# Hybrid encoder block: the output projection's weights in a pool of their own, both right-hand pools waiting tile by tile

## Chip, cores and metric

The kernel runs on one core of one Trainium2 chip. The metric is the time of one execution on the device, in microseconds (us); the figure before is the median of three runs.

## What is computed

One layer of a streaming encoder over 2,048 tokens with 16 learned tokens ahead of them, width 1,024, float32. Three groups of heads read the same normalised input: a gated linear recurrence, a forgetting attention (8 heads of 64) and an RWKV-7 recurrence. Their outputs are put side by side and go through one output projection; a feed-forward part follows.

```python
p = rms_norm(h, norm_mix_pre) @ w_in
mixed = concatenate([rg_lru(p[a]), forgetting_attention(p[b]), rwkv7(p[c])]) @ w_out
h = h + rms_norm(mixed, norm_mix_post)
f = causal_dwconv(rms_norm(h, norm_ffn_pre) @ ffn_up, ffn_conv)
gate, val = split(f)
h = h + rms_norm((gelu(gate) * val) @ ffn_down, norm_ffn_post)
```

## The kernel before

The program is traced in the order of the code, and a scheduler puts each engine's instructions into one fixed order; at run time each engine follows its row of instructions and waits with semaphores. All loads and stores of this part are issued by SP, in one row.

The stages follow each other: input projection with the recurrences beside it (to about 1120 us), forgetting attention (about 900 to 1540 us), output projection (from 1200 us beside the attention, to 1650 us), feed-forward up (to about 2460 us) and down.

**Attention** (class `Attn`, L446 to L860). A step is one head and 512 queries. `maxima` (L542) multiplies queries with keys into `mx` (L566), and VectorE reduces each `mx` to maxima (L571); this runs two steps ahead of the rest. `weights` (L661) computes the scores `sc` (L693, L694), ScalarE makes the exponentials `p` out of them (L698, nine buffers), TensorE multiplies them with the values into `po` (L716), and POOL (GpSimd) adds them up in `acc` (L737, two buffers; each fourth addition is VectorE's). At the end of a step `acc` is split (L769, L770), summed over the partitions on TensorE (L772, L773), copied to its first row (L774), and SP writes that row of 512 denominators to DRAM (L775, `scr_den<-acc`). It comes back as a small tile `dcol` (L776), is inverted, written (L781) and read as `rb` (L782); the scaled output is written to `scr_mix` (L786). So an `acc` is free for the step after next when its L775 has left it.

**Output projection.** `w_out_load` (L1508) loads the weights, already split into two halves of float32r (`woh` and `wol`), with sixteen loads of 512 KB. `w_out_tile` (L1519) takes one tile of tokens: `load_parts` (L163) loads the mixed heads into `raw` (L167), ScalarE rounds them to `mh` (L168), VectorE takes the rest `ml` (L169), and `mm3` (L172) multiplies in three products (L174 to L176) into `pswo`. The first tile (tile 0) has only two tokens. Tiles 0 to 6 run beside the attention; tiles 7 and 8 are held behind the step before the last of the attention.

**Memory.** SBUF is given out from both sides. On the right lie, during the first stage, the recurrences' buffers (`gp`, `rp`). During the attention a tile `pad` of 95,488 bytes a partition, which nothing writes, holds that place, and the attention's last tiles (`mt`, `k2`) lie further in. When `pad`'s pool is closed, `g_post` (4 KB a partition) and the pool `wp` are laid from the right edge: `woh` and `wol` (32 KB each), `mh` and `ml` (two of 4 KB each), `raw` (4 KB), `wx` (two of 4 KB) and smaller ones, in all some 5 KB more than `pad` with `g_post` counted in. A pool that is opened plainly waits as a whole for everything that lay in its place before; one opened with `early` (`reuse_waits: "tile"`) has each tile wait only for what lay in that tile's own place.

Of the kernel before, what the change touches and what calls it, by code (L numbers as in the profile page):

```python
# [329 lines left out]
def scratch(tc, ctx, core):  # L330
    dr = ctx.enter_context(tc.tile_pool(name="scr", bufs=1, space=DRAM))
    scr = {
        "p": dr.tile([A_ROWS + C_ROWS, PAD + T], F32, name="scr_p"),
        "v": dr.tile([T, 512], F32, name="scr_v"),
        "f": dr.tile([8, T], F32, name="scr_f"),
        "ch": dr.tile([8, T], F32, name="scr_ch"),
        "cl": dr.tile([8, T], F32, name="scr_cl"),
        "den": dr.tile([8, T], F32, name="scr_den"),
        "rden": dr.tile([8, T], F32, name="scr_rden"),
        "mix": dr.tile([D, T], F32, name="scr_mix"),  # L340
        "h": dr.tile([T, D], F32, name="scr_h"),
        "ff": dr.tile([FF, SEQ], F32, name="scr_ff"),
        "part": dr.tile([SEQ, D], F32, name="scr_part"),
        "us": dr.tile([NFF, P, 4 * 512], F32, name="scr_us"),
        "wo": dr.tile([KD, 2, P, D], F32, name="scr_wo"),
        "wk": dr.tile([3 * D // P + 1, 2, P, D], F32, name="scr_wk"),
        "ds": dr.tile([DOWN_PAIRS, P, 4 * 512], F32, name="scr_ds"),
    }
    for s in ("qh", "ql", "kh", "kl"):
        scr[s] = dr.tile([512, T], F32, name="scr_" + s)  # L350
    return scr
# [1156 lines left out]
def w_out_load(core, pool, scr):  # L1508

    nc = core.nc  # L1510
    wh = pool.tile([P, KD, D], F32R, tag="woh", name="woh", bufs=1)
    wl = pool.tile([P, KD, D], F32R, tag="wol", name="wol", bufs=1)
    for k in range(KD):
        for i, t in enumerate((wh, wl)):
            nc.sync.dma_start(t[:, k].bitcast(F32), scr["wo"][k, i])
    return wh, wl
# [578 lines left out]
def hybrid_block_kernel(ctx: ExitStack, tc: tile.TileContext, args, out):  # L2095
    a = {s: v[0] if s != "meta_tokens" else v for s, v in args.items()}
    nc = tc.nc
    core = Core(tc, ctx)
    scr = scratch(tc, ctx, core)
# [8 lines left out]
    def pool(es, name, bufs, **kw):  # L2108
        return es.enter_context(tc.tile_pool(name=name, bufs=bufs, **kw))

    right = {"side": "right"}
    early = {"reuse_waits": "tile"}

    def spread(pl, vec, name):
        t = pl.tile([P, D], F32, tag=name, name=name)
        nc.sync.dma_start(t[:], vec.rearrange("(o n) -> o n", o=1).broadcast_to([P, D]))
        return t
# [3 lines left out]
    with ExitStack() as p1:  # L2121
# [65 lines left out]
        p2 = ExitStack()  # L2187
# [9 lines left out]
    with ExitStack() as p3:  # L2197
        ps_n = pool(p3, "ps_n", 2, space=PSUM, **early)
        ps_f = [pool(p3, "ps_f0", 3, space=PSUM, **early)]
        np_ = pool(p3, "np", 3, **early)  # L2200
        tmp = pool(p3, "tmp", RAWS, **early)
        g_fpre = spread(gf, a["norm_ffn_pre"], "g_fpre")
        uw = [pool(p3, "uw0", UWA, **early)] * UWA
        xo = [pool(p3, f"xo{i}", 1, **early) for i in range(3)]
        tiles = [
            [(i, f, r) for i, (f, r) in enumerate(FFN_TILES) if f < FBLK * 2 * s + FBLK + FN and f + r > FBLK * 2 * s]
            for s in range(SUPERS)
        ]
        rs = {}
        with p2:  # L2210
            ps_wo.append(pool(p2, "ps_wo2", 1, space=PSUM, **right))

            banks = Banks(core, [(ps_f[0], "up", 3), (ps_wo[0], "wo", 2), (ps_wo[1], "wo", 1)])
            g_post = spread(pool(p2, "gpost", 1, **right), a["norm_mix_post"], "g_post")
            wp = pool(p2, "wp", 2, **right)
            core.apart = True
            w = w_out_load(core, wp, scr)
            todo = list(tiles[0])
            quarters = {0: ffn_quarters(core, qp, 0)}
            for i, (f, rows) in enumerate(FFN_TILES):  # L2220
                with tc.issue_after(at.steps[-2].ins) if i in HELD else nullcontext():
                    rs[i] = w_out_tile(
                        core, wp, banks, scr, w, x, meta, g_post, f + META - HALO, rows,
                        rsv[:, 6 * i : 6 * i + 6] if i < len(FFN_TILES) - 1 else None,
                        (core.acted, at.reduced) if i == HELD[-1] + 1 else (),
                    )
                banks.wide = core.root = i >= LATE - 1
                core.apart = not core.root
                if i == LATE:
                    with tc.issue_after(core.finished.ins):  # L2230
                        at.later.pop()[2]()
                for _ in range(NORMS if i > LATE else 0):
                    if todo:
                        q, f, rows = todo.pop(0)
                        xt = ffn_fetch(core, np_, scr, f, rows)
                        ffn_norm(core, ps_n, xt, f, rows, rs[q], g_fpre, quarters[0], 0)
                        if not todo:
                            run(ffn_sums(core, quarters[0]))
        ps_f.append(pool(p3, "ps_f1", 3, space=PSUM, **early))
        uw += [pool(p3, "uw1", UWB, **early)] * UWB  # L2240
        xo += [pool(p3, f"xo{i}", 1, **early) for i in range(3, XO)]
        up = pool(p3, "up", 2, **early)

        sums, ws, down, fetched = [iter(())], {}, [], []

        def fetch():
            if todo:
                q, f, rows = todo.pop(0)
                fetched.append((q, f, rows, ffn_fetch(core, np_, scr, f, rows)))

        def slot():
            down.append(down.pop(0))
            home = down[-1]
            return home.tile([P, 2, 512], F32R, tag="dw", name=core.n("dw")) if hasattr(home, "tile") else home

        def between(sup, j):

            for _ in range(1 + (j % 4 == 3) if sup else 0):
                next(later, None)
            sup += 1  # L2260
            if j == 1 and sup < SUPERS:
                quarters[sup] = ffn_quarters(core, qp, sup)
                todo[:] = tiles[sup]
                fetch()
            elif j == 1:
                kept = qp.tile([P, DOWN_KEPT, 2, 512], F32R, tag="q", name=core.n("qd"))
                down.extend(kept[:, i] for i in range(DOWN_KEPT))
                down.append(gf.tile([P, 2, 512], F32R, tag="g_fpre", name=core.n("kd"))[:])
            elif sup == SUPERS:
                if j in DOWN_FROM:  # L2270
                    raw = lambda: tmp.tile([P, 512], F32, tag="uq", name=core.n("raw"))[:]
                    k = DOWN_FROM.index(j)
                    some = range(min(len(DOWN_PRODUCTS), len(down) - len(DOWN_PRODUCTS) * k))
                    ws[k] = down_operands(core, raw, slot, a["ffn_down"], scr, k, some)
            elif fetched:
                q, f, rows, xt = fetched.pop(0)
                fetch()
                behind = lambda: tc.issue_after(core.conved.ins)
                if rs[q] is None:
                    junk = ps_n.tile([P, 512], F32, tag="mm", name=core.n("psj"))  # L2280
                    v = rsv[:rows, 6 * q : 6 * q + 6]
                    sums_ = v[:, 4:5], v[:, 5:6]
                    for half, acc in enumerate(sums_):
                        with tc.issue_after(core.taken.ins):
                            nc.scalar.activation(
                                junk[:rows], xt[:rows, 512 * half : 512 * half + 512], AF.Square, accum_out=acc
                            )
                    with behind():
                        rs[q] = rstd_root(core, v, sums_, D)
                ffn_norm(core, ps_n, xt, f, rows, rs[q], g_fpre, quarters[sup], sup, behind)  # L2290
                if not fetched:
                    sums.append(ffn_sums(core, quarters[sup], lambda: tc.issue_after(core.pooled.ins)))
            else:
                for _ in range(2):
                    next(sums[-1], None)

        later = down_sums(core, tmp, a["ffn_down"], scr, lambda: tc.issue_after(core.pooled.ins))
        ffn_up(
            core, tmp, uw, up, ps_f, a["ffn_up"], cw, scr, between,
            lambda sup, i: ffn_operand(core, xo, quarters[sup], i),  # L2300
        )
# [78 lines left out]
```

## Time and profile before

| | |
|---|---|
| runs (three) | 2991.94, 2995.55, 2996.49 us |
| median | 2995.55 us |
| span of the profiled execution | 2994.3 us |
| PE busy in the span | 2898.0 us (97%) |
| granted TensorE clock, mean | 0.976 |
| first weight load of the output projection issued | 1166.72 us |
| first matmul of the output projection | 1199.97 us |

Times in the profile count from the start of the span. PE is TensorE's matmuls, PEld its weight loads, DVE is VectorE, ACT ScalarE, POOL GpSimd, SPq the queue of SP. A line such as L716 is the line of the kernel; the tile names have their numbers left out. In a timeline a row begins with its start and its duration, and the bracket at its end has the idle time of the engine before it and what ended that. The profiled execution's own time isn't listed beside its span; the span lies inside the runs.

### The profile page before, as it was taken

Reading aid. Unit: us, or ns where it says so; the run is one execution under the profiler, and the core shown is the slowest. Engines: PE = TensorE matmul, PEld = TensorE weight load, DVE = VectorE, ACT = ScalarE, POOL = GpSimd, SP = SyncE. Lnnn points to the kernel's source line nnn. Section 1 sums busy time; section 2 is a strip of 40 time slices with the busy share of each in tenths; the row PEclk is TensorE's granted clock in tenths of the full one; section 3 lists DMA queues with packets and bytes.
Section 4 is the critical chain, followed back from the end, with each engine's and each line's share of the span. In section 5 each row is a group of like instructions: output and inputs, shape, how many; then the busy total and the mean of one; then the engine's idle time right before and its main releaser. Section 6 shows DMA issues by size and latency. Waiting matters only on the chain.

```text
span 2994.3 us, 52802 instructions
## 1 busy us (share of the span) xinstructions
PE 2898.0 (97%) x18694; PEld 2486.3 (83%) x18694; DVE 2037.0 (68%) x3937; ACT 1480.8 (49%) x2858; POOL 1319.7 (44%) x1567
## 2 busy tenths in 40 slices
PE   6999999999999999999999999999999999999998
PEld 6998899888886655665568999999999999787887
DVE  5258644765677776565636998898778787656766
ACT  4246332443346554455634656666565665424333
POOL 1002122121223665666843667446655544656443
PEclk9999899999988999999999999999999999999999
DMA  6777469676644347544336565577777764436453
GB/s 210 239 235 226 135 230 310 203 242 194 199 129 101 95 109 208 134 113 109 77 96 212 183 198 179 173 220 211 208 208 218 222 198 128 158 116 220 145 174 120
DMA packets 469190, 530.49 MB, mean 177 GB/s; under 512 B 85710, under 2 KB 355736, under 8 KB 467372
## 3 DMA queue, kind: packets, MB, share of 16 engines
q1 hardware_dynamic: 468156, 526.17, 58.2%
q8 instruction: 147, 2.41, 0.3%
q0 software_dynamic: 768, 0.93, 0.1%
q14 instruction: 119, 0.97, 0.1%
HBM read 368.07 MB, written 158.90 MB: 176 GB/s over the span
## 4 chain that ended last, share of the span: by engine, by line
PE 59%; DVE 4%; POOL 2%; DMA 2%; ACT 2%; issue 2%; SPq 0%; DVEq 0%; POOLq 0%; ACTq 0%
PE psu L174 9%; PE psu L175 9%; PE psu L176 9%; PE po L716 4%; PE psd L174 4%; PE psd L175 4%; PE psd L176 4%; PE mx L566 2%; PE pswo L174 2%; PE pswo L176 2%; PE pswo L175 2%; PE sc L693 2%; PE sc L694 2%; POOL acc L737 1%; DVE mc L571 1%
## 5 line engine op out<-in xcount | busy, mean ns | idle before, releaser
L175 PE MATMUL psu<-xo,uw 128*128 128x344 f32 x1848 | 591.4, 320 | 0.0
L174 PE MATMUL psu<-xo,uw 128*128 128x344 f32 x1848 | 586.0, 322 | 2.7 <-ACT u L1828 1.2
L176 PE MATMUL psu<-xo,uw 128*128 128x344 f32 x1848 | 581.9, 320 | 1.3 <-POOL uw L1657 1.0
L174 PE MATMUL psp<-xh,wh 128*128 128x384 f32 (+2 forms) x1152 | 380.8, 331 | 0.0
L176 PE MATMUL psp<-xh,wl 128*128 128x384 f32 (+2 forms) x1152 | 378.0, 328 | 0.0
L175 PE MATMUL psp<-xl,wh 128*128 128x384 f32 (+2 forms) x1152 | 377.8, 328 | 0.0
L1657 DVE TENSOR_TENSOR uw<-uq,uw 128x512 fp32r<-128x512 f32 x341 | 320.3, 944 | 59.2 <-ACT uw L1656 56.7
L174 PEld LDWEIGHTS psu<-xo,uw 128*128 128x128 f32 x1848 | 345.8, 188 | 4.3 <-DVE vb L1848 1.8
L176 PEld LDWEIGHTS psu<-xo,uw 128*128 128x128 f32 x1848 | 345.7, 188 | 2.1 <-POOL uw L1657 1.3
L175 PEld LDWEIGHTS psu<-xo,uw 128*128 128x128 f32 x1848 | 347.1, 188 | 0.0
L1656 ACT ACTIVATE uw<-uq 128x512 fp32r<-128x512 f32 x462 | 287.9, 627 | 95.7 <-PE psu L176 44.4
L698 ACT ACTIVATE p<-sc,bias 128x512 f32<-128x512 f32 (+4 forms) x352 | 197.9, 590 | 142.3 <-PE sc L694 119.2
L571 DVE TENSOR_REDUCE mc<-mx 128x1 f32<-128x512 f32 (+6 forms) x352 | 190.0, 565 | 113.6 <-PE mx L566 80.1
L1796 DVE SCALAR_TENSOR_TENSOR uy<-psu,ffn_cols,uy 128x342 f32<-128x342 f32 (+1 forms) x390 | 220.4, 567 | 61.4 <-ACT uy L1794 59.7
L1804 POOL TENSOR_TENSOR uy<-uy,uy 128x342 f32<-128x342 f32 (+1 forms) x132 | 146.5, 1110 | 229.2 <-DVE uy L1796 55.9
L737 POOL TENSOR_TENSOR acc<-acc,p 128x512 f32<-128x512 f32 (+3 forms) x208 | 222.7, 1073 | 48.4 <-DVE acc L737 23.4
L1657 POOL TENSOR_TENSOR uw<-uq,uw 128x512 fp32r<-128x512 f32 x121 | 184.4, 1524 | 133.8 <-ACT uw L1656 116.0
L174 PEld LDWEIGHTS psp<-xh,wh 128*128 128x128 f32 x1152 | 220.1, 191 | 8.7 <-issue 7.3
L176 PEld LDWEIGHTS psp<-xh,wl 128*128 128x128 f32 x1152 | 220.1, 191 | 7.0 <-issue 5.1
L175 PEld LDWEIGHTS psp<-xl,wh 128*128 128x128 f32 x1152 | 220.1, 191 | 5.0 <-issue 3.2
L1657 DVE TENSOR_TENSOR fo<-u,fo 128x896 fp32r<-128x896 f32 x88 | 101.6, 1155 | 133.7 <-ACT fo L1656 133.2
L1656 ACT ACTIVATE fo<-u 128x896 fp32r<-128x896 f32 x88 | 81.2, 923 | 206.6 <-PE psd L176 118.1
(488 smaller groups left out, 6409.4 us busy)
## 6 DMA issues: line engine op xcount, KB each, us to landing
uq<-scr_us SPq DMA_DIRECT2D x220, 256.0 KB
uq<-in_ffn_up_dram SPq DMA_DIRECT2D x209, 256.0 KB
wl<-scr_wk SPq DMA_DIRECT2D x48, 512.0 KB
wh<-scr_wk SPq DMA_DIRECT2D x48, 512.0 KB
u<-scr_ff SPq DMA_DIRECT2D x88, 256.0 KB
scr_ff<-uy SPq DMA_DIRECT2D x110, 171.0 KB
raw<-in_w_in_dram SPq DMA_DIRECT2D x24, 512.0 KB
scr_wk<-wh SPq DMA_DIRECT2D x24, 512.0 KB
```

Of the source, the lines that this page charges most:

```text
L174: nc.tensor.matmul(out, ah, bh, start=first, stop=False, skip_group_check=more)
L175: nc.tensor.matmul(out, ah, bl, start=False, stop=False, skip_group_check=more)
L176: nc.tensor.matmul(out, al, bh, start=False, stop=last, skip_group_check=more)
L566: nc.tensor.matmul(ps[:rows, : e - a], q3[:, qo : qo + rows], k2[:, a:e], start=True, stop=not last)
L571: self.reduced = nc.vector.tensor_reduce(mc[:rows, i, ci : ci + 1], ps[:rows, : e - a], axis=AX.X, op=ALU.max)
L698: last = nc.scalar.activation(p[:rows, :w], ps[:rows, :w], AF.Exp, bias=bias[:rows, j : j + 1])
L716: mm = nc.tensor.matmul(po[at : at + 64, c0:n], v1[:rows, j], p[:rows, : n - c0], start=start and i < 2, stop=end and i + 2 >= len(group), ...
L737: eng.tensor_tensor(a, ps_[0][0][:rows, c0:n] if start and i == 1 else a, p[:rows, : n - c0], op=ALU.add)
L1656: core.nc.scalar.activation(hi, src, AF.Copy)
L1657: (eng or core.nc.vector).tensor_tensor(lo, src, hi, op=ALU.subtract)
L1796: core.conved = stt(y[:, :n], src[:, i : n + i], cw[:, 44 * i + cc : 44 * i + cc + 1], y[:, :n], op0=ALU.mult, op1=ALU.add)
L1804: core.pooled = nc.gpsimd.tensor_tensor(v[:, :n], g[:, :n], v[:, :n], op=ALU.mult)
```

## The change

The weights get a pool `woh` of their own, laid right behind `g_post`, and both it and `wp` wait tile by tile.

```diff
             g_post = spread(pool(p2, "gpost", 1, **right), a["norm_mix_post"], "g_post")
-            wp = pool(p2, "wp", 2, **right)
+            wo = pool(p2, "woh", 1, **right, **early)
+            wp = pool(p2, "wp", 2, **right, **early)
             core.apart = True
-            w = w_out_load(core, wp, scr)
+            w = w_out_load(core, wo, scr)
```

The sizes stay the same. What changes is what the loads wait for, and with it the order that the scheduler finds. On SP's row of DMA issues, at the place behind `g_post`, stood before (`den` holds denominators, `rb` and `dcol` are their way back, `v`, `q` are values and queries of coming steps):

```order
L2116 DMA g_post<-in_norm_mix_post_dram 128x1024
L782 DMA rb_12986<-scr_rden 64x512
L782 DMA rb_13057<-scr_rden 64x512
L775 DMA scr_den<-acc_12884 1x512
L776 DMA dcol_13044<-scr_den 16x32
L786 DMA scr_mix<-o_12734 64x512
L535 DMA v_1455_11124<-scr_v 128x16x64
L536 DMA v_1455_11124<-scr_v 16x64
L553 DMA q_1446_11103<-scr_qh 64x512
L775 DMA scr_den<-acc_13128 1x512
```

The same place on SP in the changed kernel, from the second `rb` on:

```order
L782 DMA rb_13057<-scr_rden 64x512
L1515 DMA woh<-scr_wo 128x1024
L1515 DMA wol<-scr_wo 128x1024
L1515 DMA woh<-scr_wo 128x1024
L1515 DMA wol<-scr_wo 128x1024
L1515 DMA woh<-scr_wo 128x1024
L1515 DMA wol<-scr_wo 128x1024
L1515 DMA woh<-scr_wo 128x1024
L1515 DMA wol<-scr_wo 128x1024
L775 DMA scr_den<-acc_12884 1x512
```

Eight loads stand ahead of the write of `acc_12884`; the other eight follow behind it, without any row between them. Behind those SP goes on so, to the operand of the first output tile (`raw`):

```order
L553 DMA q_1446_11103<-scr_qh 64x512
L786 DMA scr_mix<-o_12734 64x512
L775 DMA scr_den<-acc_13128 1x512
L786 DMA scr_mix<-o_12818 64x512
L776 DMA dcol_13044<-scr_den 16x32
L652 DMA scr_mix<-mt_13273 64x8x16
L535 DMA v_1455_11124<-scr_v 128x16x64
L536 DMA v_1455_11124<-scr_v 16x64
L553 DMA q_1451_11114<-scr_qh 64x512
L776 DMA dcol_13144<-scr_den 16x32
L167 DMA raw_16463<-scr_mix 128x8x2
```

So the second row of denominators (`acc_13128`) now stands behind all sixteen loads, and `raw` behind it and a load of values.

On TensorE the two orders part behind the last product of the 16 learned tokens (L635). Before, the row goes on with scores:

```order
L635 MATMUL mx_13194<-mt_12912,mt_12913 16x16
L693 MATMUL sc_13311<-q_1974_12943,k_1448_11109 128x512
L694 MATMUL sc_13311<-q_1457_11129,k_1963_12902 128x512
L566 MATMUL mx_13179<-k_1963_12902,q_1446_11103 128x512
L693 MATMUL sc_13316<-q_1974_12943,k_1448_11109 128x512
L694 MATMUL sc_13316<-q_1457_11129,k_1963_12902 128x512
```

In the changed kernel the same score, `sc_13311`, follows after 19 other rows of TensorE, maxima (`mx`) of coming steps among them; the last of those rows are:

```order
L566 MATMUL mx_13297<-k_1449_11110,q_1451_11114 128x512
L566 MATMUL mx_13304<-k_1449_11110,q_1451_11114 128x400
L566 MATMUL mx_13341<-k_1449_11110,q_1451_11114 128x384
L568 LDWEIGHTS identb
L568 MATMUL mx_13341<-futureb,identb 128x128
L566 MATMUL mx_13338<-k_1449_11110,q_1451_11114 128x512
L693 MATMUL sc_13311<-q_1974_12943,k_1448_11109 128x512
L694 MATMUL sc_13311<-q_1457_11129,k_1963_12902 128x512
```

Maxima have moved ahead of scores. Counted from behind that L635, the first output matmul (`pswo`) stands after 78 rows of TensorE in place of 182. POOL's row keeps its order here: the first sum `acc_13237<-p,p`, which takes the place of `acc_12884`, stands behind the same additions in both. From output tile 7 on to the end of the output projection TensorE's row is the same in both; in the feed-forward part some groups of matmuls change places.

## Prediction

> **What bounds the kernel now.** I read the page first. Matmuls fill the span, and the chain that ended last runs on the same engine:
>
> ```profile
> span 2994.3 us, 52802 instructions
> PE 2898.0 (97%) x18694; PEld 2486.3 (83%) x18694; DVE 2037.0 (68%) x3937; ACT 1480.8 (49%) x2858; POOL 1319.7 (44%) x1567
> PE 59%; DVE 4%; POOL 2%; DMA 2%; ACT 2%; issue 2%; SPq 0%; DVEq 0%; POOLq 0%; ACTq 0%
> ```
>
> The edit adds and removes no matmul, so it can act only through idle time of PE (TensorE). Next I cut the span into stretches around the moved loads (columns: stretch, length, then busy time of PE, PEld, DVE, ACT, POOL, granted clock, DMA share, GB/s):
>
> ```profile
> 1150.00:1200.00 50.00, 48.49 (x244) 27.02 (x241) 34.44 (x68) 30.59 (x54) 38.01 (x41) 1.00 0.78 246
> 1200.00:1500.00 300.00, 297.38 (x1352) 178.76 (x1351) 185.08 (x365) 160.48 (x289) 214.78 (x285) 1.00 0.45 107
> 1500.00:1550.00 50.00, 44.18 (x184) 26.60 (x184) 12.68 (x25) 18.99 (x36) 29.25 (x47) 0.97 0.19 53
> 1151.00:1163.00 12.00, 12.00 (x71) 7.08 (x69) 6.50 (x15) 8.35 (x16) 9.05 (x12) 1.00 0.36 79
> 1168.00:1190.00 22.00, 20.92 (x95) 10.93 (x94) 16.34 (x30) 11.75 (x21) 17.23 (x19) 1.00 1.02 375
> ```
>
> Between 1150 and 1200 PE is idle for 1.5 us, in the 300 us behind that for 2.6 us. The DMA engines have room where the loads will go (0.36 of the DMA engines at 1151 to 1163) and full where the loads lie now (1.02, 375 GB/s). Last I read SP's queue and the engine that waits for it, POOL, in order of time (start, duration, instruction, and in brackets the idle time before it and what ended it):
>
> ```profile
> 1145.33 1.09 SPq L782 DMA_DIRECT2D rb<-scr_rden  x2
> 1146.52 0.39 SPq L775 DMA_DIRECT2D scr_den<-acc  x1
> ...
> 1166.72 0.53 SPq L1515 DMA_DIRECT2D woh<-scr_wo  x1
> 1167.30 0.42 SPq L1515 DMA_DIRECT2D wol<-scr_wo  x1
> 1167.81 0.24 SPq L775 DMA_DIRECT2D scr_den<-acc  x1
> ...
> 1184.90 0.32 SPq L1515 DMA_DIRECT2D wol<-scr_wo  x1
> 1185.49 0.84 SPq L167 DMA_DIRECT2D raw<-scr_mix  x1
> ```
>
> ```profile
> 1148.55 1.27 POOL L737 TENSOR_TENSOR acc<-p,p 128x512 f32<-128x512 f32 x1 [0.73 <-DMA scr_den<-acc]
> 1149.90 2.63 POOL L737 TENSOR_TENSOR acc<-acc,p 128x512 f32<-128x512 f32 x2
> ...
> 1159.66 1.27 POOL L737 TENSOR_TENSOR acc<-p,p 128x512 f32<-128x512 f32 x1
> ...
> 1171.97 1.28 POOL L737 TENSOR_TENSOR acc<-p,p 128x512 f32<-128x512 f32 x1 [0.49 <-DMA scr_den<-acc]
> ```
>
> The reader is to see a loop that is easily missed. There are two accumulators `acc`. POOL may start an attention step's sum only when the row of denominators of the step before last (L775, 2 KB) has left its `acc`. Issued at 1146.52 into an empty queue, that write freed POOL at 1148.55, after 2.0 us. Issued at 1167.81 behind two of the weight loads, it freed POOL at 1171.97, after 4.2 us: 1.1 us more for each load ahead. The window 1168 to 1190 gives 0.524 MB / 375 GB/s = 1.4 us for a load. So a small write on this queue waits for the bulk before it.
>
> **The change, part by part.** *The pools.* The split moves no bytes and adds no instruction; its cost is only what it moves. *The loads.* By the order of SP, the sixteen loads go from 1166.72 to 1184.90 to right behind the two rb loads of 1145.33, some 20 us earlier, and with one other row between them. Eight of them now stand ahead of the denominators' write that was issued at 1146.52, all sixteen ahead of the next one. Issuing costs nothing in itself (0.3 to 0.6 us each, SP has nothing else to do then); the cost is what is queued behind them.
>
> *First term: POOL and the exponentials.* With eight loads ahead, the write lands at 1146.5 + 2.0 + 8 x 1.1 to 1.4 = 1157.3 to 1159.7; I take 1158.9 (1.3 each). Then comes POOL's first sum (1.27 us), which frees two buffers `p`, and ScalarE's exponential of the next score, which waits for just that today:
>
> ```profile
> 1149.85 1.26 ACT L698 ACTIVATE p<-sc,bias 128x512 f32<-128x512 f32 x2 [3.38 <-POOL acc L737]
> ...
> 1150.59 0.50 PE L693 MATMUL sc<-q,k 128*128 128x512 f32 x1 [0.43 <-ACT p L698]
> ...
> 1199.97 0.39 PE L174 MATMUL pswo<-woh,mh 128*2 128x512 f32 x1
> ```
>
> So the score that PE does at 1150.6 today goes to 1158.9 + 1.3 + 0.7 = 1160.9. What has PE in the meantime? In the changed order 19 rows stand ahead of that score and 78 rows ahead of the first matmul of the output projection; before, that was 0 and 182. I price them by columns moved, a `po` matmul (fp32 operands, two records each in the trace) twice: the 182 rows move 87,900 columns in the 48.5 busy us of 1150 to 1200, 0.55 ns a column. The 78 rows move 33,600, so 18.6 us; the first 19 of them 5,300, so 2.9 us. From 1150.1 PE would be through the 19 rows at 1153.0 and would stand before the score until 1160.9: 7.9 us idle.
>
> *Second term: the clock.* One longer stall of PE is in the neighbourhood:
>
> ```profile
> 1115.89 0.40 PE L694 MATMUL sc<-q,k 128*128 128x512 f32 x1
> 1119.50 0.36 PE L1345 MATMUL rps<-ident,rwxu 64*128 64x64 f32 x1 [3.21 <-DVE rwxu L1338]
> ...
> 1120.24 0.77 PE L693 MATMUL sc<-q,k 128*128 128x512 f32 x1
> 1120.81 0.63 PE L694 MATMUL sc<-q,k 128*128 128x512 f32 x1
> ...
> 1123.96 2.71 PE L716 MATMUL po<-p,v 128*64 128x512 f32 x10
> 1126.59 0.50 PE L693 MATMUL sc<-q,k 128*128 128x512 f32 x1
> 1120.00:1130.00 10.00, 8.87 (x31) 5.00 (x31) 1.72 (x11) 5.53 (x12) 4.84 (x6) 0.70 0.42 76
> 1151.94 1.74 PE L716 MATMUL po<-p,v 128*64 128x512 f32 x10
> ```
>
> After 3.2 us without work the second matmul of a score takes 0.63 us and not 0.40, ten `po` records 2.71 and not 1.74 us, and the granted clock is 0.70 over ten us. Two score pairs (0.6 us each), the `po` group (1.0) and the small ones (0.5) make 2.7 us lost. I add 2.7 us; the bounds are 0 (the stall may be cut into small ones by single maxima) and 3.0 (ten us at a clock of 0.70). The Trainium skill, "TensorE: Matmul & The Clock Gate", What's actually happening, says that one idle window of about 3.4 us halves the clock and that about 3.4 us of sustained work restores it. By that rule the term would be an estimated 1.7 us and the sum 1.0 us lower; the trace agrees in kind, with slow matmuls for longer than one such window.
>
> *Third term: the remaining rows and the first output tile.* The other 59 rows are 15.7 us of work; with 2.7 us for the clock, from 1160.9, PE reaches the output projection at 1179.3. Its operand is the `raw` load of 8 KB, which SP now issues behind the sixteen loads and behind a load of values `v`. The sixteen end at 1146.5 + 2.0 + 16 x 1.1 to 1.4 = 1166 to 1171. The `v` load lies in the window 1151 to 1163 today: 0.36 x 12 = 4.3 us of the engines, and the small pieces of `raw` a few more, so 1172 to 1178. It is covered by the scores, barely; ScalarE's split of it (`mh`, 0.2 us) stands ahead of exponentials, so where the cover fails, they wait too. I count nothing here and 0 to 2 us in the range.
>
> *Fourth term: what idle time of before goes.* The 1.5 us between 1150 and 1200. The end of the attention keeps its 5.8 us (1500 to 1550): PE's order is the same from output tile 7 on, and these tiles are held behind the last attention steps. Between tiles 0 and 7 the output matmuls only trade places with scores in a stretch that is 99% busy. In the feed-forward stages a few matmul groups change places where PE is at 100%; I count nothing.
>
> The sum: without a stall 78 rows end at 1150.1 + 18.6 = 1168.7; they end at 1179.3; 10.6 - 1.5 = +9.1 us. The profiled execution's span, 2994.3 us, lies 1.3 us under the median of the three runs, 2995.55; I add to the median: 3004.6 us. Bounds of this case: with 1.1 us a load and no clock term 10.6 - 1.6 - 2.7 - 1.5 = +4.8; with 1.4 us a load, 3.0 for the clock and 2.0 for the operand it is 10.6 + 0.8 + 0.3 + 2.0 - 1.5 = +12.2. That is 3000.4 to 3007.8. The next denominators' write, behind all sixteen, lands at 1146.5 + 2.0 + 16 x 1.3 = 1169.3; POOL, 10.4 us late, is ready for it at 1159.66 + 10.4 = 1170.1, so I count nothing for it.
>
> **The rivals.** *The small write slips by* (not slower, beyond what is measurable). Its place is L775 behind eight loads: if the engines mixed transfers piece by piece, it would land in 2 to 4 us. Then only the changed order costs: among the 19 rows stand eight maxima, and VectorE needs for each
>
> ```profile
> L571 DVE TENSOR_REDUCE mc<-mx 128x1 f32<-128x512 f32 (+6 forms) x352 | 190.0, 565 | 113.6 <-PE mx L566 80.1
> ```
>
> 0.565 us, 4.5 us in all and about 2.9 us of other work, so PE stands till 1157.5 and not till 1160.9: idle 1157.5 - 1150.1 - 2.9 = 4.5 us, less 1.5 is +3.0 us, 2998.6 us; if maxima hide too, -1.5, 2994.0 us. The point from which this decides is a landing before about 1155.6 (1157.5 less 1.9 for sum and exponential). Against it speak the 4.2 us behind two loads. The Trainium skill, "DMA: Bandwidth & Descriptors", Queues, rings and completion order, adds that a queue's descriptors are consumed in ring order on each engine, which speaks against this rival and against the change; no row of before has eight loads ahead of a write.
>
> *Faster.* The end of the attention loses its waits: if steps pulled in by the earlier output tiles gave POOL and VectorE slack there, 5.8 + 1.5 = 7.3 us would go, 2988.3 us. For it: those waits are for VectorE's and POOL's sums. Against it: the same rows in the same order there, and a stretch without output matmuls that gets longer by 72 rows.
>
> *Worse.* The operand of tile 0 and then that of tile 1 arrive late, ScalarE stands before each with exponentials queued behind, and the clock falls twice: 9.1 + 3 + 2.7 + 2 = +17, 3012 us.
>
> *The edit does nothing.* Not so: the loads do move in the order.
>
> **How the numbers follow.** A measurement of this kernel can tell about 0.2%, 6.0 us. The forecast has 0.60 (of which 0.09 lies under 6 us), the write that slips by 0.25, faster 0.08, worse 0.07. Slower by over 0.2%: 0.51 + 0.07 = 0.58. Within 0.2%: 0.25 + 0.09 = 0.34. Faster: 0.08. The range takes in the likeliest case and the first rival, 2994.0 to 3007.8, and on the upper side the 1.3 us between median and span, 3009; it leaves out the two others (0.15).
>
> **What would show it.** Right: the first `woh` load at about 1146.5; POOL's `acc<-p,p` of 1148.55 at 1157 to 1160, released by the DMA of the denominators; a stall of PE of some us before a score just ahead of that; the first `pswo` matmul at 1175 to 1181; PE's idle time between 1150 and 1200 near 11 us and unchanged behind 1500. Wrong: POOL's sum starting before 1155.6, or PE as busy as before between 1150 and 1200 (then the first rival); PE's idle time at 1500 to 1550 under 3 us (then the faster one).

## The result and the profile after

Four runs of the changed kernel took 3001.86, 3005.66, 3016.70 and 3017.80 us, median 3011.18; four of the kernel before beside them 2995.11. The ratio is 1.0058, with a 95% interval of 1.0035 to 1.0080: slower by some 16 us, where the prediction had 9.1. Two executions among the experiments below, 12426.36 us in held and 6685.50 us in burst2, took more than twice as long as any other and are left out of the ratios.

The profiled execution is the fastest of the four (span 3000.2 us). It was ahead before the two orders part: by 2.4 us at the first matmul of the input projection (39.8 us against 42.2), by 3.7 at the start of its last products (873.8 against 877.5), by 6.5 at the first `po` (910.0 against 916.5) and by 7.5 at the last L635 (1142.53 against 1149.99). Up to there PE has the same rows in both. One difference on the way is the granted clock at 870 to 1120 us. Before, then after (columns as in the prediction: stretch, length, busy time of PE, PEld, DVE, ACT, POOL, granted clock, DMA share, GB/s):

```profile
870.00:1120.00 250.00, 231.62 (x2023) 158.90 (x2022) 189.13 (x518) 136.25 (x297) 130.80 (x205) 0.87 0.45 105
```

```profile
870.00:1120.00 250.00, 226.45 (x2019) 152.99 (x2017) 189.45 (x520) 138.91 (x300) 133.83 (x208) 0.90 0.45 106
```

The clock was 0.90 and not 0.87 there, and PE busy 5.2 us less; but it was idle 5.2 us more, so the clock is not shown to be the cause of the head start, and what is stays open. Comparing spans would hide 7.5 us of the change, so everything below is compared by stretches between the same matmuls. First the attention, from the last L635 to the last `po`; then the rest of the output projection, to the first `psu`; then feed-forward up, from the first to the last `psu`. Before:

```profile
1149.99:1538.36 388.37, 380.45 (x1737) 225.16 (x1734) 227.34 (x446) 206.22 (x372) 277.91 (x362) 1.00 0.46 117
1538.36:1645.92 107.56, 105.53 (x493) 86.73 (x493) 61.70 (x104) 45.89 (x109) 30.99 (x34) 1.00 0.62 203
1645.92:2538.44 892.52, 888.56 (x5641) 885.95 (x5639) 737.17 (x1122) 561.41 (x1106) 492.32 (x384) 1.00 0.66 195
```

After:

```profile
1142.53:1540.99 398.46, 384.76 (x1737) 227.31 (x1734) 227.52 (x446) 205.92 (x372) 277.62 (x363) 0.98 0.44 111
1540.99:1649.34 108.35, 106.32 (x493) 86.79 (x494) 61.79 (x104) 45.89 (x109) 31.04 (x34) 1.00 0.62 202
1649.34:2544.69 895.35, 889.95 (x5641) 888.28 (x5639) 733.34 (x1122) 562.61 (x1106) 494.16 (x384) 1.00 0.66 195
```

The stretches are longer by 10.1, 0.8 and 2.8 us: 13.7 together. Less the head start of 7.5 us, and the 0.4 us that the down stage takes less, that is the 5.9 us by which the spans differ. The length of a stretch (388.37 us in the first row) less the busy time of PE is PE's idle time: in the attention 13.7 us after, 7.9 before. As the matmuls are the same, the 4.3 us more of busy time are matmuls at a lower clock.

The chain that was predicted is there, row by row. SP's queue, then POOL, ScalarE and PE (start, duration, instruction, in brackets the idle time before it and its end):

```profile
1138.16 0.58 SPq L1515 DMA_DIRECT2D woh<-scr_wo  x1
...
1141.96 0.45 SPq L1515 DMA_DIRECT2D wol<-scr_wo  x1
1142.52 0.28 SPq L775 DMA_DIRECT2D scr_den<-acc  x1
```

```profile
1150.85 1.27 POOL L737 TENSOR_TENSOR acc<-p,p 128x512 f32<-128x512 f32 x1 [5.23 <-DMA scr_den<-acc]
```

```profile
1152.15 1.26 ACT L698 ACTIVATE p<-sc,bias 128x512 f32<-128x512 f32 x2 [3.03 <-POOL acc L737]
```

```profile
1152.89 0.80 PE L693 MATMUL sc<-q,k 128*128 128x512 f32 x1
1170.81 0.40 PE L174 MATMUL pswo<-woh,mh 128*2 128x512 f32 x1
```

And the stretches from the last L635 to these two:

```profile
1142.53:1152.89 10.36, 8.44 (x42) 4.89 (x38) 6.72 (x16) 2.31 (x5) 2.54 (x3) 0.66 1.02 410
1142.53:1170.81 28.28, 25.34 (x114) 14.05 (x111) 16.51 (x38) 11.55 (x23) 14.20 (x17) 0.82 0.93 329
```

The denominators' write, issued behind eight loads, frees POOL after 8.3 us (2.0 before). The score follows 10.4 us behind the last L635, the first output matmul 28.3 us behind it. But PE does not stand in between: it is idle for 1.9 us of the 10.4. For the other 8.4 us it works on the rows that now stand ahead of the score, priced at 2.9 us in the prediction, at a mean granted clock of 0.66. Behind 1500 us nothing changed:

```profile
1500.00:1550.00 50.00, 44.09 (x186) 25.75 (x187) 14.48 (x26) 20.22 (x38) 31.97 (x47) 1.00 0.16 45
```

### The profile page after: what moved, and what is told of

Same layout as the page of the kernel before. It is cut to its first block, busy times and chain, and to the rows that moved or that the text cites. A ratio compares the mean times of both kernels' runs of the same rounds, so it can differ in the third digit from the quotient of the medians.

```text
span 3000.2 us, 52800 instructions
## 1 busy us (share of the span) xinstructions
PE 2892.2 (96%) x18694; PEld 2480.8 (83%) x18694; DVE 2033.1 (68%) x3937; ACT 1481.4 (49%) x2858; POOL 1322.0 (44%) x1567
## 4 chain that ended last, share of the span: by engine, by line
PE 78%; DVE 8%; DMA 6%; ACT 3%; POOL 3%; issue 2%; SPq 1%; DVEq 0%; POOLq 0%; ACTq 0%
PE psu L174 9%; PE psu L175 9%; PE psu L176 9%; PE psp L174 5%; PE psp L176 5%; PE psp L175 5%; PE psd L174 4%; PE psd L175 4%; PE psd L176 4%; PE po L716 4%; PE pswo L174 2%; PE mx L566 2%; PE pswo L176 2%; PE pswo L175 2%; PE sc L693 2%
```

## The experiments

**Theory 1** is the prediction's: what stands ahead of the small writes on SP's queue costs. **Theory 2**: the feed-forward stages, or the new order of the rows as such. **Theory 3**: the pools' places. Ratios are against the kernel before, run on the same chip in the same rounds, with their 95% intervals; the times in the expectations take that kernel at about 2995 us, while on the chip of spread, behind, upfirst and swap its median was 2990.2, and on that of burst and spreadup 2990.0. The table has each kernel's attention stretch, PE's idle time in it, and feed-forward up, taken from one trace each as above. The ratio's interval says whether a kernel as a whole is slower than the kernel before; the stretches say where.

| kernel | ratio | interval | attention, us | idle, us | up, us |
|---|---|---|---|---|---|
| before / once more | | | 388.4 / 389.1 | 7.9 / 8.5 | 892.5 / 892.4 |
| changed | 1.0058 | 1.0035–1.0080 | 398.5 | 13.7 | 895.4 |
| again | 1.0050 | 1.0031–1.0069 | 395.4 | 13.6 | 895.6 |
| wlfirst (same rows) | one run | | 398.6 | 13.7 | 896.0 |
| burst | 1.0045 | 1.0029–1.0062 | 399.2 | 15.0 | 895.6 |
| burst2 | 1.0014 | 1.0002–1.0026 | 389.0 | 9.4 | 892.4 |
| spread | 1.0032 | 1.0018–1.0046 | 389.6 | 10.1 | 895.9 |
| behind | 1.0035 | 1.0020–1.0051 | 398.7 | 14.9 | 896.5 |
| poolq | 1.0113 | 1.0086–1.0140 | 402.9 | 21.6 | 896.1 |
| actq | 1.0080 | 1.0062–1.0098 | 395.5 | 15.4 | 895.4 |
| held | 1.0034 | 1.0019–1.0050 | 394.2 | 15.0 | 896.7 |
| swap | 1.0024 | 1.0010–1.0038 | 398.6 | 14.6 | 893.6 |
| swaphold | 1.0016 | 1.0002–1.0031 | 391.3 | 8.9 | 896.1 |
| upfirst | 1.0035 | 1.0019–1.0051 | 398.4 | 13.5 | 892.2 |
| spreadup | 1.0011 | 1.0002–1.0020 | 391.2 | 10.3 | 893.0 |

**Do the stretches repeat?** again is the changed kernel unchanged, beforeb the kernel before.

> The changed kernel once more, for its scatter and a second trace. Every theory: 3002 to 3018 us, median near 3011, against 2992 to 2997 for the kernel before. Theory 1 (the sixteen loads ahead of the small denominators' write hold POOL, ScalarE and then PE, and the clock falls behind the stall): PE needs some 28 us from the end of the row matmuls at L635 to the first pswo, with a granted clock under 0.8 in ten of them, whatever the run's time. Theory 2 (the feed-forward stages, whose matmul groups change places, lose the time): the stretch from the first psu to the last is 3 us or more longer than before, in which 6 to 10 us of the 16 are found where the run is slow.

> The kernel before once more, for a second trace. If its stretch from L635 to the last po is set by its order, 387 to 390 us again with some 7.8 us of gaps; if the first trace was a lucky one, 392 us or more, by low clock of 3.4 us at a time. The first psu's wait for xo is under 1.5 us again.

again took 3001.71 to 3015.26 us, median 3008.43; beforeb 2991.46 us in its one run. The idle times repeat within 0.6 us; the attention of the changed order moves by 3 us (395.4 and 398.5), with the granted clock (0.99 and 0.98 in that stretch). So idle time belongs to the order, and part of the clock to chance. No single trace of one kernel settles 3 us.

**Loads ahead of the write, in the kernel before.** burst keeps the old pools and the late loads, and adds eight loads whose data nothing reads (shortened; in its trace, lines behind the addition count up by one or nine, L775 is L776):

```diff
+            self.burst()                       # in total(), ahead of L775
+    def burst(self):
+        self.dens = getattr(self, "dens", 0) + 1
+        if self.dens == 14:
+            with self.core.tc.issue_after(self.rbs.ins):     # the last rb load
+                for j in range(8):             # burst2: range(2)
+                    self.nc.sync.dma_start(self.pad[:, 1024*j : 1024*j+1024], self.scr["wo"][j//2, j%2])
```

> The kernel before, with its pools and its late loads, and eight loads of 512 KB more, into a tile that nothing reads, put where the change has the first eight: behind the two rb loads and ahead of the denominators' write of acc_12884. It adds work that the reference doesn't need. Theory 1 (what stands ahead of that write costs, whatever the pools): the write lands some 8 us after its issue, and the stretch from the last L635 matmul to the last po matmul takes 393 to 398 us, not 388.4; 5 to 10 us slower than the kernel before. Theory 3 (the pools' new places cost, the bytes ahead of the write do not): 388 to 390 us, at most 2 us slower.

> The kernel before with two loads of 512 KB more (into a tile that nothing reads) ahead of the denominators' write of acc_12884, not eight; TensorE's rows are those of the kernel before but for some twenty beside the score that waits for this write. Theory 1 (each load ahead of the write costs in proportion): the write lands some 4 us after its issue, and the stretch from the last L635 matmul to the last po takes 390 to 392 us; 1.5 to 4 us slower than the kernel before. Theory 2 (the re-ordered rows cost, the delay does not): 388 to 389.5 us, within 1.5 us of it. With eight loads it was 399.2 us and some 13 us slower.

SP, POOL and the attention's stretch of burst:

```profile
1137.45 4.34 SPq L805 DMA_DIRECT2D pad<-scr_wo  x8
1142.23 0.24 SPq L776 DMA_DIRECT2D scr_den<-acc  x1
```

```profile
1151.88 1.27 POOL L737 TENSOR_TENSOR acc<-p,p 128x512 f32<-128x512 f32 x1 [4.92 <-DMA scr_den<-acc]
```

```profile
1143.88:1543.03 399.15, 384.15 (x1737) 226.93 (x1734) 233.34 (x446) 205.10 (x372) 279.29 (x363) 0.98 0.47 121
```

Eight loads ahead of the write, with the pools of the kernel before, give all of the attention's loss: 399.2 us, 15.0 idle, the write after 9.7 us. For the attention theory 3 falls. The time, 0.45% or 13.5 us, is more than the 5 to 10 that were expected, for its feed-forward up is longer by 3.1 us as well. There PE waits for VectorE's `vb` for 3.4 us in all (0.9 in the kernel before; the line has total, times, longest), with a granted clock of 0.91 in the 20 us around the longest of these waits:

```profile
PE psu L174 <- DVE vb L1857: 3.4, 4, 2.3
```

Two loads delay the write to 3.0 us (some 4 were expected), and the stretch takes 389.0 us with 9.4 idle: in the range of theory 2 (388 to 389.5), not of theory 1 (390 to 392). The time shows 0.14%, 4 us, more than theory 2 had and just clear of nothing. So the cost is not in proportion to the loads. What burst cannot separate is the delay from the order: the scheduler knows of the delay and moves maxima ahead of the score here too.

**The loads in parts, or right behind the write.** Both are the changed kernel with handles on the denominators' writes (`at.dens[13]` is that of `acc_12884`, 14 that of `acc_13128`; shortened):

```diff
-            w = w_out_load(core, wo, scr)
+            with tc.issue_after(at.dens[13].ins):              # behind
+                w = w_out_load(core, wo, scr)
+            # spread: k = 0, 1 at once; k = 2, 3 behind dens[13]; k = 4..7 behind dens[14]
```

> Early loads as in the change, in three parts: four ahead of the denominators' write of acc_12884, four behind it, eight behind that of acc_13128. Theory 1: with four loads ahead the write lands 5 to 6 us after its issue, half of the changed kernel's delay: the stretch from L635 to the last po takes 391 to 394 us, 3003 to 3007 us, between the two others. Theory 2 (the order of the rows decides): no graded answer to the number of loads ahead; 394 us or more and 3006 to 3011 us.

> Early loads in the pool of their own as in the change, but the first of them is issued right behind the denominators' write of acc_12884 and not eight loads ahead of it; the next such write stands behind eleven of them. Feed-forward as in the change. Theory 1 (the write behind the loads holds POOL and then PE): this write lands 2 us after its issue, POOL's sum starts within 3 us of it, and the stretch from the last L635 matmul to the last po matmul takes 389 to 393 us (before 388.4, changed 395 to 398): 3001 to 3005 us. Theory 2 (any other order of the attention's rows costs as much, as in the kernel with held loads): the write is on time and the stretch takes 394 us or more: 3006 to 3011 us.

In spread the write is issued at 1142.41 and frees POOL at 1147.69, 5.3 us, as expected; the attention takes 389.6 us with 10.1 idle, less than theory 1 gave it. In behind the write is on time and the stretch still takes 398.7 us: theory 1's numbers failed, and theory 2's (the write on time, 394 us or more) came true. Its SP and POOL:

```profile
1144.90 0.25 SPq L775 DMA_DIRECT2D scr_den<-acc  x1
1164.47 0.39 SPq L775 DMA_DIRECT2D scr_den<-acc  x1
```

```profile
1146.71 1.28 POOL L737 TENSOR_TENSOR acc<-p,p 128x512 f32<-128x512 f32 x1
1166.35 1.27 POOL L737 TENSOR_TENSOR acc<-p,p 128x512 f32<-128x512 f32 x1
```

The first write is on time, 1.8 us. The second, behind eleven loads, is issued 19.6 us after the first, where the kernel before has 9.5 (1146.52 and 1156.05), and POOL's second sum is late by as much. So the delay was moved to the second write. That this is what costs PE its time is not shown: from the last L635 to the wait for the first output matmul, at 1180.00, PE has no wait of 0.4 us. Its longest waits are for that tile's operand `mh` and, in all of 1140 to 1545 us, for VectorE's reductions (total, times, longest; 1.9 us for these before):

```profile
PE pswo L174 <- ACT mh L168: 2.3, 1, 2.3
PE mx L566 <- DVE mc L571: 5.9, 11, 1.6
```

Nor does the count of loads ahead of a small write decide alone. In spread four stand ahead of the first write, four more ahead of the second and eight ahead of the third; POOL begins the sum that follows the third without a wait for it, 9.2 us after its issue, and the attention is 1.2 us longer than before:

```profile
1165.38 0.39 SPq L775 DMA_DIRECT2D scr_den<-acc  x1
1174.57 1.28 POOL L737 TENSOR_TENSOR acc<-p,p 128x512 f32<-128x512 f32 x1
```

So eight loads ahead of a write did little here, where POOL was not yet waiting for it.

**Another queue.** L1515 issued by GpSimd (`nc.gpsimd.dma_start`, poolq) or ScalarE (`nc.scalar.dma_start`, actq).

> The changed kernel with the sixteen loads issued by GpSimd on a queue of its own in the place of SP's; early as in the change. Theory 1a (the write waits for its queue's order): the denominators' write on SP's queue lands 2 to 3 us after its issue, POOL's acc<-p,p is not released late, PE has no low clock behind; 2995 to 3001 us, if the sixteen issues cost POOL no more than some 0.5 us each. Theory 1b (the DMA engines are full, whatever the queue): the write still lands 6 us or more after its issue and the time is 3006 to 3013 us. Theory 2 (feed-forward): at least 3001 us with the write on time.

> The changed kernel with the sixteen loads issued by ScalarE on its queue in the place of SP's. Theory 1a (queue order): the denominators' write lands 2 to 3 us after its issue and POOL starts on time; but each load takes a place in ScalarE's row of exponentials, and one that waits for its semaphore holds the exponentials behind it: 2996 to 3003 us. Theory 1b (full DMA engines): the write lands 6 us or more after its issue; 3006 to 3014 us. Theory 2 (feed-forward): at least 3001 us with the write on time.

Both are slower than the change. On a row of their own the loads go out still earlier (poolq from 1129.18, actq from 1119.3 us), onto the loads of keys and queries. A part of their loss lies ahead of the last L635, outside the table's stretch: in poolq PE waits 7.2 us at 1140.51 for POOL's `k` (keys). In poolq, DMA (in a stretch of 30 us around the write, then between its issue and POOL's sum) and the write:

```profile
1135.00:1165.00 30.00, 20.50 (x85) 11.11 (x85) 18.94 (x42) 3.22 (x7) 8.14 (x15) 0.67 1.04 298
1160.81:1170.37 9.56, 2.57 (x25) 1.31 (x25) 2.36 (x6) 0.79 (x2) 0.01 (x1) 0.73 0.76 216
```

```profile
1160.81 0.22 SPq L775 DMA_DIRECT2D scr_den<-acc  x1
```

```profile
1170.37 1.26 POOL L737 TENSOR_TENSOR acc<-p,p 128x512 f32<-128x512 f32 x1 [11.32 <-DMA scr_den<-acc]
```

The write is on SP's queue and the weights are not, and still it takes 9.6 us; the DMA engines were full in the 30 us (1.04) and busy to 0.76 between its issue and POOL's sum. Theory 1a's numbers fall. Its queue order is not excluded: SP had issued bulk of its own ahead of the write, the 512 KB of `g_post` at 1152.30 and 128 KB of queries at 1155.96. The Trainium skill, "DMA: Bandwidth & Descriptors", Queues, rings and completion order, says that each engine takes turns between the queues, packet by packet. Whether that helped here no run shows, because of that bulk on the write's own queue. In actq, ScalarE stands 15.3 us at the issues before one small activation, and PE waits 6.1 us at 1131.52, ahead of the last L635 too.

**The pools with late loads.** held keeps the change and holds the loads behind the store they stood behind before (`with tc.issue_after(...)` on L652's store). swap makes the two pools in the other order:

```diff
-            wo = pool(p2, "woh", 1, **right, **early)
             wp = pool(p2, "wp", 2, **right, **early)
+            wo = pool(p2, "woh", 1, **right, **early)
```

swaphold is swap with the `wx` loads (L1531) behind the last weight load (shortened):

```diff
-    nc.sync.dma_start(xt[:rows], ...)
+    with core.tc.issue_after(core.wloaded.ins):
+        nc.sync.dma_start(xt[:rows], ...)
```

> Own pools for the loads and for the feed-forward weights as in the change, but the sixteen loads are held behind the store that they stood behind before (L652), so they go out some 20 us later again; the feed-forward stages have the changed kernel's order row by row. Theory 1 (the loads' early place costs all of it): 2993 to 2998 us, the denominators' writes land within 2 to 4.5 us of their issue, no clock under 0.9 in the ten us behind. Theory 2 (pools and feed-forward order cost part of it): 3001 to 3006 us. Theory 3 (they cost all of it, and the early loads are hidden): 3009 to 3013 us.

> The two pools of the change, both waiting tile by tile, made in the other order: the loads' pool lies at another address, the loads stand again within two rows of where they stood before, the rows of the attention up to the first output tile are those of before, and the fourth xo does not wait. Theory 1 and the xo's wait together make up all of the loss: 2993 to 2998 us. Theory 3 (a pool of its own, or waiting tile by tile, costs by itself; or any other order of rows does): 3000 to 3008 us.

> The two pools of the change, waiting tile by tile, in the other order, and the wx loads of the output projection, which slipped ahead of the denominators' write there, held behind the weights' loads: SyncE's queue and TensorE's rows of the attention are those of the kernel before. Theory 1 (what stands ahead of the small writes): the 10 us of the stretch from L635 to the last po, 398.6 us in the swapped kernel, go down to 388 to 390, and the time to within 2 us of the kernel before. Theory 3 (own pools cost by themselves): the stretch stays over 393 us and the time 5 to 8 us above.

swap lost 10 us in the attention though its weights load late. Its trace shows a wait even for one load ahead of the write: SP, POOL, PE.

```profile
1139.00 0.37 SPq L1531 DMA_DIRECT2D wx<-in_x_dram  x1
1139.46 0.23 SPq L775 DMA_DIRECT2D scr_den<-acc  x1
```

```profile
1142.86 1.26 POOL L737 TENSOR_TENSOR acc<-p,p 128x512 f32<-128x512 f32 x1 [2.88 <-DMA scr_den<-acc]
```

```profile
1144.89 0.50 PE L693 MATMUL sc<-q,k 128*128 128x512 f32 x1 [2.60 <-ACT p L698]
```

Here the 512 KB load of `wx` has slipped ahead of the same write, which frees POOL after 3.4 us, and PE stands 2.6 us before the score. That isn't the whole 10 us. PE stands another 2.3 us at a later score, for which ScalarE is late: it splits the `mh` of an output tile first, and stood before that for `raw`. The granted clock of the ten us behind is 0.66:

```profile
1217.89 1.06 ACT L168 ACTIVATE mh<-raw 128x1024 fp32r<-128x1024 f32 x1 [3.93 <-DMA raw<-scr_mix]
1219.58 0.50 PE L693 MATMUL sc<-q,k 128*128 128x512 f32 x1 [2.34 <-ACT p L698]
```

burst2, with two loads ahead of the same write, lost 0.6 us of the stretch; so one load there is not shown to cost 10. With `wx` held, SP's and PE's rows of the attention are those of the kernel before, in the change's own pools:

```profile
1147.52:1538.77 391.25, 382.38 (x1737) 225.65 (x1734) 227.29 (x446) 205.48 (x371) 276.65 (x362) 0.99 0.45 116
```

The idle time is 8.9 us, within 1 us of the kernel before (7.9 and 8.5); the 2 us left are clock (0.99). So pools of their own cost PE no waiting in the attention once the rows are those of before. The stretch (388 to 390 expected) and the time were missed all the same: 1.0016 overlaps swap's, and the hold changed the feed-forward's order too (896.1). held speaks against theory 1 as the whole account. Its loads stand only five rows earlier than before, three ahead of the third write where there were two, and yet PE idles 15.0 us: 6.6 for VectorE's reductions (1.6 before, over the same stretch) and 2.9 for one row of ScalarE's. There the new order costs though the loads are late.

**Feed-forward.** The fourth `xo` (the split input of the up product) is the first buffer laid where the right-hand pools were. In the kernel before nothing delays its split on ScalarE; in the changed one it waits for the last output tile and stands behind three later `xo`:

```
before:  L1656 xo_3145<-q   (no wait)   row 1397, then xo_3150, xo_3156, xo_3161
changed: L1656 xo_3145<-q   waits for five DMA semaphores, VectorE, ScalarE   row 1407, behind those three
```

upfirst changes the places of the later pools, spreadup adds that to spread:

```diff
+        up = pool(p3, "up", 2, **early)
         uw += [pool(p3, "uw1", UWB, **early)] * UWB
         xo += [pool(p3, f"xo{i}", 1, **early) for i in range(3, XO)]
-        up = pool(p3, "up", 2, **early)
```

> The changed kernel with the feed-forward's later pools placed in another order (up, uw1, xo3 on, in the place of uw1, xo3 on, up): the buffer of the fourth xo no longer lies over a buffer of the last output tile. Every instruction up to the end of the attention stays where the change has it. Theory 2 (the feed-forward loses because this xo waits): the 4.48 us wait of the first psu matmuls for xo goes, with it the low clock behind it, and the stretch from the first to the last psu takes 892 to 893 us, not 895.5: 3004 to 3007 us, 3 to 4 below the changed kernel. Theory 1 alone (all in the attention): no change, 3008 to 3011 us.

> The loads in three parts among the denominators' writes and the feed-forward's later pools in the other order, both as in the kernels measured apart. If the two costs are two: the stretch from L635 to the last po takes 389 to 392 us as with the loads in parts, that from the first to the last psu 892 to 893 us as with the other pools, and the time is 3 to 4 us below that with the loads in parts: 4 to 6 us above the kernel before. If they are one, or trade against each other: no gain over either, 9 to 11 us above the kernel before. No theory has it faster than the kernel before: PE does not wait for the loads in either.

PE's first wait in feed-forward up in the changed kernel, the windows around and right behind it, and then upfirst's whole stretch:

```profile
1659.67 1.17 PE L174 MATMUL psu<-xo,uw 128*128 128x344 f32 x2 [4.47 <-ACT xo L1656]
```

```profile
1650.00:1660.00 10.00, 5.53 (x34) 5.20 (x33) 9.23 (x11) 9.08 (x15) 2.56 (x1) 0.89 0.31 105
1660.00:1670.00 10.00, 10.00 (x50) 9.80 (x50) 9.38 (x10) 4.79 (x10) 6.48 (x5) 0.77 0.42 133
1659.67:1664.63 4.96, 4.96 (x16) 4.71 (x17) 4.96 (x5) 3.06 (x6) 1.39 (x1) 0.50 0.41 122
```

```profile
1657.28:2549.44 892.16, 885.73 (x5641) 883.85 (x5639) 735.81 (x1122) 564.53 (x1106) 490.02 (x384) 1.00 0.65 195
```

The wait of 4.47 us is gone with the overlap, and so is the half clock behind it, which cost 2.5 us (4.96 busy us at 0.50); the stretch takes 892.2 us, as before. Its attention, row by row the changed kernel's, keeps its 398.4. So the pools' places cause the 2.8 us. The wait explains them only in part: PE idles 6.4 us of upfirst's stretch, 5.4 of the changed kernel's and 4.0 of the one before, because other waits take its place; upfirst's gain lies in 4.2 us less of busy time, 1.7 of them not explained by that clock. Its time, 1.0035 against 1.0058 and 1.0050 of the changed kernel, fits, but the intervals overlap. spreadup has both cures: 391.2 and 893.0 us, 1.0011. That is one third of spread's loss and a fifth of the change's, and 4 to 6 us above the kernel before was expected (4.0 measured): the two costs are two and add up. It is the best version of the early loads, and not faster than the kernel before, in which PE does not wait for these loads at all.

**The output matmuls' pace.** wlfirst allocates `wol` ahead of `woh`.

> The changed kernel with the low half of the weights allocated ahead of the high half, so that both lie at other addresses; every engine's rows are those of the changed kernel. The output projection's matmuls of 512 columns, 0.227 us apart in the kernel before, are 0.229 us apart in the changed one. If that comes from where these weights lie, the distance changes; if from where the activations (mh, ml) lie, it stays at 0.229.

Its output stretch has 106.32 us of busy PE, as the changed kernel's, not 105.53: which half lies first is not the cause.

## Why the prediction was wrong

It forecast 3004.6 us with a range to 3009.0; 3011.2 lies above it. Two of the four runs lie inside the range, and so does the median of again, 3008.43.

- *The landing of the write.* Predicted 8.9 us behind the last L635 (1158.9 against 1150.0), measured 8.3. Right.
- *First and second term and the idle time given back, +9.1 us.* The attention's stretch is longer by 10.1 us (again: 7.0; wlfirst: 10.2). Near in size, and burst shows that bulk at that place is the cause; whether by the write's delay or by the order that the scheduler makes for it stays open. That the sum came out near is partly luck, since its terms did not. It had 7.9 us of a standing PE before the score and 2.7 us of a low clock behind that stall, less 1.5 us given back. Measured are 5.8 us more of idle time and 4.3 of clock. The step "PE would be through the 19 rows at 1153.0" failed: these rows kept PE busy for 8.4 us and not 2.9, and the clock fell during them, ahead of the score and not behind it. Nor was the place right. Up to the first output matmul PE idles 2.9 us (before 1.5); behind it 10.8 and not 6.4:

```profile
1170.81:1540.99 370.18, 359.41 (x1624) 213.26 (x1623) 211.01 (x410) 194.37 (x350) 263.42 (x347) 1.00 0.40 95
```

```profile
1199.97:1538.36 338.39, 331.98 (x1495) 198.17 (x1494) 192.92 (x379) 175.61 (x318) 239.89 (x321) 0.99 0.41 98
```

  The step "between tiles 0 and 7 the output matmuls only trade places with scores in a stretch that is 99% busy" was wrong by 4.4 us. They trade places with maxima too, and PE then waits longer for VectorE's reductions. PE's waits for them at 1140 to 1545 us, before and after (total, times, longest):

```profile
PE mx L566 <- DVE mc L571: 1.9, 5, 0.8
```

```profile
PE mx L566 <- DVE mc L571: 4.8, 6, 1.4
```

- *Third term, 0.* Right: `raw` was issued at 1165.24 and split without a wait at 1168.84. The rival in which that operand is late did not happen, though its 3012 us lie near the result.
- *The end of the attention, 5.8 us.* Right: 5.9.
- *The step that failed: "in the feed-forward stages a few matmul groups change places where PE is at 100%; I count nothing".* It was +2.8 us (3.1 and 3.4 in again and wlfirst). upfirst shows that the later pools' places cause it: one `xo` waits for the last output tile, PE for it, and the clock falls. The order was seen to change, but a busy share was read in place of the wait at the stage's first rows. With this term the sum would have been 3007.4 us, inside the range.
- *Counted by no step:* the output matmuls' slower pace, 0.8 us.

Terms measured: 10.1 + 0.8 + 2.8 = 13.7 us. The two medians differ by 16.1, and again's ratio gives 15.0. The rest is within the scatter: the four runs of the changed kernel lie 16 us apart, and those of the kernel before went from 2981.92 to 3004.64 us on other chips. The range was drawn round one anchor of three runs, with no room for that.

## What to carry to other kernels

Before bulk loads are moved earlier, list the small transfers that pass through the same queue and the same engines in that stretch, and who waits for each, and when. Eight loads ahead of a write that POOL was waiting for came with 7 to 11 us of loss in the attention (the changed kernel, burst); in parts of four, four and eight ahead of three such writes (spread, spreadup) they came with 1.2 and 2.8. An order of rows that the scheduler finds anew can cost as much with that write on time (behind, held), so read each engine's waits in the new order too. A pool's place is a wait: where buffers of the next stage lie over those just split off, look at that stage's first rows for a new one. When the granted clock moves runs by several us, compare stretches between the same matmuls, and read idle time and busy time apart.

## What was not expected of the hardware

The clock fell without a long wait. PE's longest idle time between 1142.5 and 1155 us was 1.38 us, and yet the granted clock of the ten us from 1145 on was about a half. The last two lines are the 3.4 us ahead of the fall and the stretch at half clock:

```profile
1145.67 1.58 PE L644 MATMUL mx<-mt,mt 16*64 16x16 f32 x14 [1.38 <-DVE mc L559]
```

```profile
1145.00:1150.00 5.00, 4.05 (x23) 2.60 (x23) 1.52 (x4) 0.68 (x1) 0.58 (x1) 0.58 1.03 416
1150.00:1155.00 5.00, 4.93 (x12) 3.16 (x12) 3.98 (x10) 1.95 (x3) 3.81 (x3) 0.50 1.02 405
1142.39:1145.80 3.41, 1.83 (x20) 0.91 (x17) 3.18 (x9) 0.89 (x2) 0.58 (x1) 1.00 1.01 404
1145.80:1156.04 10.24, 9.90 (x38) 6.00 (x39) 5.58 (x10) 3.27 (x5) 4.11 (x4) 0.50 1.03 413
```

PE was busy 9.0 of these ten us, so the delay looks like slow matmuls and hardly like a wait. At the wait of 4.47 us at the first `psu` the clock of 0.89 and 0.77 in ten us each makes 6.8 us at half (1.1 and 2.3 us lost, at 0.50): the half clock began some 2.6 us into the wait, and the 4.96 us of it behind the wait cost 2.5 us. The Trainium skill, "TensorE: Matmul & The Clock Gate", What's actually happening, gives an idle window of about 3.4 us as what throttles, and a free-running window. In neither case had PE been idle for 3.4 us when the clock fell: 1.6 us of idle time in the 3.4 us ahead of the first fall, and some 2.6 us of wait ahead of the second. There the measurement decides, and no threshold comes out of it: at the end of the attention a wait of 2.2 us stands in both kernels, and the clock of 1500 to 1550 us is 0.97 before and 1.00 after.

The output matmuls take the same 493 records of PE in 106.32 us in the kernels with the weights' pool right behind `g_post`, and in 105.53 us in the kernel before, swap and burst. PE's rows are the same in this stretch and the granted clock is 1.00 in all of these (swaphold and spreadup, at 0.98, are left aside); the places of the weights and activations in memory differ, and so do some rows of the other engines. What makes the 0.7% stays open.
